# First down operands in the up weights' tiles, token sums ahead of a norm, and rows scaled on VectorE in an fp32 encoder block

## The chip, the cores and the metric

The kernel runs on one core of a Trainium2 chip. TensorE (PE in the profile) multiplies, VectorE (DVE) and ScalarE (ACT) do the elementwise work, GpSimd (POOL) raises the sums of the norms to a power, and SyncE's queue (SP) issues nearly all transfers between HBM and the core's memory. The metric is the device time of one execution, in microseconds (us).

## The reference

One encoder block on 2048 tokens of 1024 numbers, with 16 meta tokens ahead of them, all in fp32 (depth 1):

```python
for i in range(DEPTH):
    hn = rms_norm(h, g_mix[i])
    proj = hn @ w_in[i]                       # q, k, v and u, 512 + 256 + 256 + 512 wide
    ...                                       # axial rope, attention, Fourier mixing
    mixed = concatenate([rms_norm(attn, g_attn_out[i]), rms_norm(four, g_fourier_out[i])])
    h = h + mixed @ w_out[i]
    m = rms_norm(h, g_mlp[i])
    h = h + square(relu(m @ w_up[i])) @ w_down[i]      # 1024 -> 4096 -> 1024
return rms_norm(h, g_final)[:, N_META:]
```

## The kernel before

Every fp32 product is made of three matmuls on two halves of each operand: `split` writes hi, a cast on ACT (L64), and lo, the rest, a subtraction on DVE (L65); `mm3` then issues hi by hi (L74), one cross product (L75) and the other (L76). An operand of 128x1024 numbers is one cast and one subtraction.

The tokens stand in four blocks of 512. First come the projections, the Fourier part and attention; the MLP of blocks 0 and 1 is interleaved with attention (`head`, `up`, `down`), its weights coming through `wtile`: a ring of raw tiles (wr), and rings of four hi (wh) and four lo (wl) tiles. Blocks 2 and 3 are done last and together, each of the two products of the MLP as a Strassen scheme of seven forms, whose order is `ORDER = "1265734"`:

- `flip` scales the rows of blocks 2 and 3 by their norm (L1128), transposes them on PE (L1132) and evicts them (L1133) into b11, b21, b12, b22. Form operands bf1 to bf7 are splits of these four and of sums of them; bf3 to bf7 lie in a pool `sl` that takes the place of the pools `mp` and `wp`, and so over the rows of block 1.
- `final(1)` norms block 1 (DVE, L1036, with rs from POOL) and stores it to out.
- the up stage: 8 groups g of 512 columns of w_up, in each 7 forms of 24 matmuls (ux, uy in PSUM); the weights of a form come from `up_weights` (raw tiles R0 and R1, sums us1 and us2, halves wuh and wul, all in pool `sp`). Copies p1, p5, p6 (ACT, L1219) and sums c, s make the squared activations, which SP stores to s_d in HBM.
- the down stage: 4 groups of 7 forms of 48 matmuls (dx, dy). `down_operands` loads s_d (raw a) and w_down (raw d11, d21, d12, d22) and splits them into rings of five (ah, al, bh, bl). Sums d11 and t2 come between. DVE adds each finished product to hs (L1356), the rows of blocks 2 and 3. At the end each row is normed with g_final (gf) and stored.

A scheduler orders each engine's instructions; each engine then runs in its order, and SP's queue issues in its own, waiting with each DMA for the one eight before it. A tile that takes the place of another waits for that one's last readers, its store included.

Of the kernel before, what the change touches and what calls it, by code (L numbers as in the profile page):

```python
# [129 lines left out]
def encoder_block(ctx: ExitStack, tc: tile.TileContext, x, meta, w_in, w_f,  # L130
# [893 lines left out]
    def final(b):  # L1024
        b0, n = BLOCKS[b]
        hs = H.pop(b)
        gfin = load_gfin(b)
        for t in range(2 * n):
            ss = MT[b, "f"][t]
            sm = mp.tile([P, 1], F32, name=f"fsm_{b}_{t}", tag="hsm", bufs=2)  # L1030
            nc.vector.tensor_tensor(sm, ss[:, 0:1], ss[:, 1:2], op=ALU.add)
            rs = rstd_of(mp, sm, 1, D, "m2" if b == 2 else "m")
            r0 = (2 * b0 + t) * P
            for i in range(2):
                v = hs[t][:, i * 512:(i + 1) * 512]
# [131 lines left out]
    bt = {n: sl.tile([P, 2, 4, 512], R32, name="bf" + n, tag="bf" + n) for n in ORDER[2:]}  # L1167
    two = (slice(0, 2), slice(2, 4))
# [313 lines left out]
```

## Time and profile before

| | |
|---|---|
| median of 3 runs | 2391.14 us (2390.89 to 2393.72) |
| profiled execution, its own time | 2395.55 us |
| its span | 2393.8 us |
| PE busy | 2324.0 us (97%) |
| DVE busy | 1748.4 us (73%) |
| ACT busy | 1302.5 us (54%) |
| POOL busy | 161.4 us (7%) |

The span runs from the first to the last instruction that the profiler saw. Matmuls are pipelined, so a row of 0.39 us starts 0.23 us after the one ahead of it. A wait in brackets is idle time of that engine just ahead of the row, with what ended it. PEclk is the share of the full TensorE clock that was granted.

### The profile page before, as it was taken

How to read it: one execution, taken by the hardware profiler on the slowest of the kernel's cores; microseconds unless marked ns; L12 is line 12 of the kernel's file. 1: busy time of each engine (PE TensorE's matmuls, PEld its weight loads, DVE VectorE, ACT ScalarE, POOL GpSimd, SP SyncE). 2: the span in 40 equal slices, each digit the busy share in tenths (PEclk: the TensorE clock that was granted, in tenths of full speed). 3: DMA queues.
4: the chain of work that ended last, by engine and by line, in shares of the span. 5: the costliest groups of instructions: out<-in, count | busy, mean ns of one | idle time of the engine just before them, and what ended most of it. 6: DMA issues, size and time to landing. Idle time of an engine off the chain costs nothing.

```text
span 2393.8 us, 33707 instructions
## 1 busy us (share of the span) xinstructions
PE 2324.0 (97%) x12326; PEld 1977.8 (83%) x12326; DVE 1748.4 (73%) x2953; ACT 1302.5 (54%) x2529; POOL 161.4 (7%) x207
## 2 busy tenths in 40 slices
PE   8999989999999999999999999999979999799998
PEld 7889889788788888888888888888868888688886
DVE  5434678998687877787887887877484656487786
ACT  6434345654666656566765665665755555433343
POOL 2212120101100000000000000000000000000000
PEclk9999999999999999999999999999989999899999
DMA  6333152434334222234242334223334445755431
GB/s 210 108 98 114 45 169 56 153 115 150 128 88 117 74 77 70 76 102 118 70 150 80 133 106 126 67 71 114 138 110 163 150 145 178 266 185 169 139 123 71
DMA packets 169446, 288.64 MB, mean 121 GB/s; under 512 B 14160, under 2 KB 63024, under 8 KB 169280
## 3 DMA queue, kind: packets, MB, share of 16 engines
q1 hardware_dynamic: 149472, 256.34, 32.6%
q0 software_dynamic: 19808, 30.15, 4.8%
q8 instruction: 97, 1.59, 0.3%
q14 instruction: 69, 0.57, 0.1%
HBM read 216.93 MB, written 69.50 MB: 120 GB/s over the span
## 4 chain that ended last, share of the span: by engine, by line
PE 76%; DVE 4%; ACT 3%; DMA 2%; issue 1%; POOL 1%; SPq 0%; POOLq 0%; DVEq 0%; ACTq 0%
PE pup L74 5%; PE pup L75 5%; PE pup L76 5%; PE pdn L74 5%; PE pdn L75 5%; PE pdn L76 4%; PE s L74 2%; PE s L76 2%; PE s L75 2%; PE ux L74 2%; PE ux L76 2%; PE ux L75 2%; PE dx L74 2%; PE dx L75 2%; PE dx L76 2%; PE o L757 2%
## 5 line engine op out<-in xcount | busy, mean ns | idle before, releaser
L74 PE MATMUL pdn<-wh_dn,ah 128*128 128x512 f32 x512 | 202.6, 397 | 0.0
L74 PE MATMUL pup<-mT,wh_up 128*128 128x512 f32 x512 | 202.0, 396 | 0.7 <-ACT mT L67 0.7
L75 PE MATMUL pdn<-wl_dn,ah 128*128 128x512 f32 x512 | 202.0, 394 | 0.0
L76 PE MATMUL pup<-mT,wl_up 128*128 128x512 f32 x512 | 201.7, 396 | 0.0
L75 PE MATMUL pup<-mT,wh_up 128*128 128x512 f32 x512 | 201.7, 394 | 0.0
L76 PE MATMUL pdn<-wh_dn,al 128*128 128x512 f32 x512 | 199.5, 392 | 0.0
L696 ACT COPY S<-s 128x512 f32<-128x512 f32 (+1 forms) x288 | 159.8, 559 | 62.7 <-PE s L76 42.4
L736 DVE TENSOR_TENSOR S<-S,mb 128x512 f32<-128x512 f32 (+1 forms) x288 | 185.9, 654 | 4.4 <-ACT mb L725 4.3
L741 ACT ACTIVATE S<-S 128x512 f32<-128x512 f32 (+1 forms) x264 | 156.0, 603 | 59.3 <-DVE S L736 58.1
L64 ACT CAST wh_up<-wr_up 128x512 fp32r<-128x512 f32 x128 | 79.4, 620 | 160.5 <-PE pdn L76 71.6
L74 PE MATMUL s<-q,kt 128*128 128x256 f32 (+1 forms) x544 | 159.2, 293 | 1.4 <-ACT S L696 1.4
L703 DVE TENSOR_TENSOR M<-M,S 128x512 f32<-128x512 f32 (+1 forms) x224 | 145.4, 649 | 14.4 <-ACT S L696 12.9
L76 PE MATMUL s<-q,kt 128*128 128x256 f32 (+1 forms) x544 | 154.9, 285 | 0.0
L75 PE MATMUL s<-q,kt 128*128 128x256 f32 (+1 forms) x544 | 154.4, 284 | 0.0
L65 DVE TENSOR_TENSOR wl_up<-wr_up,wh_up 128x512 fp32r<-128x512 f32 x128 | 87.6, 688 | 87.0 <-ACT wh_up L64 86.9
L64 ACT CAST ah<-a 128x1024 fp32r<-128x1024 f32 x56 | 58.7, 1051 | 162.1 <-issue 58.8
L65 DVE TENSOR_TENSOR wl_dn<-wr_dn,wh_dn 128x512 fp32r<-128x512 f32 x128 | 88.0, 688 | 71.6 <-ACT wh_dn L64 70.6
L64 ACT CAST wh_dn<-wr_dn 128x512 fp32r<-128x512 f32 x128 | 79.3, 619 | 105.2 <-PE pdn L76 55.9
L763 DVE TENSOR_TENSOR acc<-acc,S 128x512 f32<-128x512 f32 x168 | 115.2, 686 | 1.7 <-ACT S L741 1.7
L65 DVE TENSOR_TENSOR pl<-S,ph 128x512 fp32r<-128x512 f32 x168 | 114.6, 686 | 2.0 <-ACT ph L64 1.4
L74 PE MATMUL dx<-bh,ah 128*128 128x512 f32 x256 | 100.7, 394 | 14.3 <-ACT bh L64 14.3
L74 PE MATMUL o<-ph,vt 128*128 128x256 f32 x384 | 111.5, 290 | 2.1 <-ACT ph L64 2.0
(310 smaller groups left out, 6818.7 us busy)
## 6 DMA issues: line engine op xcount, KB each, us to landing
wr_up<-in_w_up_dram SPq DMA_DIRECT2D x128, 256.0 KB, 2.8
wr_dn<-in_w_down_dram SPq DMA_DIRECT2D x128, 256.0 KB, 2.7
a<-s_d SPq DMA_DIRECT2D x56, 512.0 KB, 3.8
R<-in_w_up_dram SPq DMA_DIRECT2D x16, 1024.0 KB, 5.5
s_d<-s SPq DMA_DIRECT2D x64, 256.0 KB, 2.0
d<-in_w_down_dram SPq DMA_DIRECT2D x32, 512.0 KB, 4.8
s_d<-c SPq DMA_DIRECT2D x48, 256.0 KB, 2.0
h<-h_d SPq DMA_DIRECT2D x20, 512.0 KB, 6.0
```

The costliest lines, as they stand in the source:

```text
L64: nc.scalar.copy(hi, src)
L65: nc.vector.tensor_tensor(lo, src, f32v(hi), op=ALU.subtract)
L74: nc.tensor.matmul(out, a[0], b[0], start=first, stop=False, skip_group_check=chain)
L75: nc.tensor.matmul(out, a[0], b[1], start=False, stop=False, skip_group_check=chain)
L76: nc.tensor.matmul(out, a[1], b[0], start=False, stop=last, skip_group_check=chain)
L696: nc.scalar.copy(S[:rows, :n], ps[:rows, :n])
L703: nc.vector.tensor_tensor(M[:rows, :n], M[:rows, :n], S[:rows], op=ALU.max)
L736: nc.vector.tensor_tensor(S, S, bc(s["mb"][:rows], [rows, n, 256]), op=ALU.subtract)
L741: nc.scalar.activation(p, S, AF.Exp, scale=ISQ)
L757: nc.tensor.matmul(s["O"], vt[t // 4][:, t % 4], p[:, e], start=t == 0, stop=False)
L763: nc.vector.tensor_tensor(acc, acc, p, op=ALU.add)
```

## The change

Three things are done. First, the operands of form 1 of the first down group are made while the last up group (g = 7) runs: the raw a1 and d11 are loaded into R0 and R1, which no further up weights need, and split into the tiles of wuh, wul, us1 and us2. Half of the rows hs is loaded during that group, too, and the gf loads stand behind the first operands' loads. The ring bh, bl of the down operands lies in a new pool `dr` over `sp`, allocated after form 1's products. Second, at the start of the up stage the sums of the token operands come ahead of `final(1)`, into an extra tile (b32 in the listings); g_final is loaded earlier, the first half of block 1's rows is multiplied by it ahead of the norm on DVE (L1163 after the change), and by rs on ACT (L1038), the second half as before on DVE (L1040). The forms are then split in the order 6, 5, 7, 3, 4. One more up form is made ahead (4 for 3). Third, `flip` scales its rows on DVE instead of ACT, and the raw weight ring has three tiles for four.

```diff
@@ in wtile (and in out_f alike)
-        raw = wp.tile([P, 512], F32, name="wr_" + name, tag="wr", bufs=4)
+        raw = wp.tile([P, 512], F32, name="wr_" + name, tag="wr", bufs=3)
@@ in final, now final(b, early=None)
-        gfin = load_gfin(b)
+        gfin = early or load_gfin(b)
...
-                nc.vector.scalar_tensor_tensor(v, v, rs, gfin[i], op0=ALU.mult, op1=ALU.mult)
+                if early and i == 0:
+                    nc.scalar.activation(v, v, AF.Copy, scale=rs)
+                else:
+                    nc.vector.scalar_tensor_tensor(v, v, rs, gfin[i], op0=ALU.mult, op1=ALU.mult)
@@ before and in flip
-    ready = [next(UW) for _ in range(3)]
+    ready = [next(UW) for _ in range(4)]
...
-            nc.scalar.activation(hs[t], hs[t], AF.Copy, scale=ms[t])
+            nc.vector.tensor_scalar(hs[t], hs[t], ms[t], None, op0=ALU.mult)
@@ the token operands
     mix2(down(1, 7, (0,)), flip(2, h2, (b11, b21)))
+    gfin = load_gfin(1)
+    for t in range(4):
+        nc.vector.tensor_tensor(H[1][t][:, :512], H[1][t][:, :512], gfin[0], op=ALU.mult)
...
-    b12, b22 = (rb.tile([P, 4, 512], F32, name=f"b{i}2", tag=f"b{i}2") for i in (1, 2))
+    b12, b22, b22t = (rb.tile([P, 4, 512], F32, name=f"b{i}2", tag=f"b{i}2") for i in (1, 2, 3))
     mix2(down(1, 7, (1,)), flip(3, H.pop(3), (b12, b22)))
     b_form("1", ...)
     b_form("2", ...)
-    final(1)
+    minus(b11, b12, b11)      # dst = a - b, in two halves
+    minus(b22t, b22, b11)
+    final(1, gfin)
     mp.release()
     wp.release()
...
-    for c in two:
-        nc.vector.tensor_tensor(b11[:, c], b12[:, c], b11[:, c], op=ALU.subtract)
-    b_form("3", bt["3"], b22)
-    for c in two:
-        nc.vector.tensor_tensor(b12[:, c], b22[:, c], b12[:, c], op=ALU.subtract)
-        nc.vector.tensor_tensor(b22[:, c], b22[:, c], b11[:, c], op=ALU.subtract)
-    b_form("6", bt["6"], b22)
-    b_form("5", bt["5"], b11)
-    b_form("7", bt["7"], b12)
-    for c in two:
-        nc.vector.tensor_tensor(b21[:, c], b21[:, c], b22[:, c], op=ALU.subtract)
-    b_form("4", bt["4"], b21)
+    b_form("6", bt["6"], b22t)
+    b_form("5", bt["5"], b11)
+    minus(b12, b22, b12)
+    b_form("7", bt["7"], b12)
+    b_form("3", bt["3"], b22)
+    minus(b21, b21, b22t)
     rb.release()
+    sl4 = Lines(tc.alloc_tile_pool(name="sl4", bufs=1, reuse_waits="tile"), small)
+    b_form("4", sl4.tile([P, 2, 4, 512], R32, name="bf4", tag="bf4"), b21)
@@ new, ahead of the up loop
+    def first_down():
+        a = sp.tile([P, 4, 512], F32, name="a1_0", tag="R0")
+        nc.sync.dma_start(a, s_d[0][:, 0])
+        w = sp.tile([P, 4, 512], F32, name="d11_0", tag="R1")
+        for h in range(2):
+            nc.sync.dma_start(w[:, 2 * h:2 * h + 2], w_down[...])
+        yield
+        for h in range(2):
+            for x, r in (("a", a), ("b", w)):
+                tags = ("us1", "us2") if h and x == "b" else ("wuh", "wul")
+                hi, lo = (sp.tile([P, 2, 512], R32, ...) for e, t in zip("hl", tags))
+                split(hi, lo, r[:, 2 * h:2 * h + 2])
+                FIRST.append((hi, lo))
+                yield
+        yield w
@@ in the up loop, after a form's matmuls are issued
+            elif g == 7:
+                next(first, None)
+                if name == "7":
+                    load_h(0)
@@ in down_operands (RING["b"] is a pool dr, made over sp after form 1 of group 0)
-            stationary("1")
-            load(1, 1)
+            if g:
+                stationary("1")
+                load(1, 1)
+            else:
+                raw[1, 1] = [w11[:, 0:2], w11[:, 2:4]]
             stationary("2")
...
-            yield form("1", raw[1, 1])
+            if g == 0:
+                t1 = [dn.tile([P, 2, 512], F32, name=f"d11_0_{h}", tag="d11", bufs=2) for h in range(2)]
+                sub(t1, raw[1, 2], raw[1, 1])
+            yield form("1", raw[1, 1]) if g else FIRST
             yield form("2", raw[2, 1])
@@ ahead of and in the down loop
-    for t in range(8):
-        nc.sync.dma_start(hs[t], h_d[8 + t])
+    DO = down_operands()
+    ready = [next(DO)]
+    load_h(1)
     gfin = ...
-    DO = down_operands()
-    ready = [next(DO) for _ in range(2)]
...
+                if "b" not in RING:
+                    sp.release()
+                    RING["b"] = dr = Lines(tc.alloc_tile_pool(name="dr", ...), small)
+                    ready.append(next(DO))
```

DVE at the end of the up stage and the start of the down stage, before (dx_0_0 is the first product of form 1 of group 0; al1, bl1 are the lo halves of form 1, al2, bl2 of form 2):

```order
L1225 TENSOR_TENSOR s4_7_1_21008<-c21_7_1_21004,s2_7_1_20965 128x512
L65 TENSOR_TENSOR al1_0_0_21060<-a1_0_0_21031,ah1_0_0_21059 128x1024
L65 TENSOR_TENSOR al1_0_1_21068<-a1_0_1_21033,ah1_0_1_21067 128x1024
L65 TENSOR_TENSOR bl1_0_0_21064<-d11_0_0_21035,bh1_0_0_21063 128x1024
L65 TENSOR_TENSOR bl1_0_1_21072<-d11_0_1_21037,bh1_0_1_21071 128x1024
L65 TENSOR_TENSOR al2_0_0_21076<-a2_0_0_21039,ah2_0_0_21075 128x1024
L65 TENSOR_TENSOR al2_0_1_21084<-a2_0_1_21041,ah2_0_1_21083 128x1024
L1356 TENSOR_TENSOR hs0_21017<-hs0_21017,dx_0_0_21099 128x512
L65 TENSOR_TENSOR bl2_0_0_21080<-d21_0_0_21043,bh2_0_0_21079 128x1024
L1356 TENSOR_TENSOR hs0_21017<-hs0_21017,dx_0_1_21112 128x512
```

And after the change:

```order
L1268 TENSOR_TENSOR s4_7_1_21038<-c21_7_1_21034,s2_7_1_20991 128x512
L1407 TENSOR_TENSOR hs0_20930<-hs0_20930,dx_0_0_21092 128x512
L1407 TENSOR_TENSOR hs0_20930<-hs0_20930,dx_0_1_21105 128x512
L1407 TENSOR_TENSOR hs0_20930<-hs0_20930,dx_0_2_21118 128x512
L65 TENSOR_TENSOR al2_0_0_21149<-a2_0_0_21051,ah2_0_0_21148 128x1024
L1407 TENSOR_TENSOR hs0_20930<-hs0_20930,dx_0_3_21131 128x512
L65 TENSOR_TENSOR al2_0_1_21157<-a2_0_1_21053,ah2_0_1_21156 128x1024
L1327 TENSOR_TENSOR d11_0_0_21071<-d12_0_0_21059,d11_0_20895 128x1024
L1327 TENSOR_TENSOR d11_0_1_21072<-d12_0_1_21061,d11_0_20895 128x1024
L1327 TENSOR_TENSOR t2_0_0_21164<-d22_0_0_21063,d11_0_0_21071 128x1024
L65 TENSOR_TENSOR bl2_0_0_21153<-d21_0_0_21055,bh2_0_0_21152 128x1024
L65 TENSOR_TENSOR bl2_0_1_21161<-d21_0_1_21057,bh2_0_1_21160 128x1024
```

The four lo halves of form 1 stood behind the last up sum (s4); now the last of them, al1_0_1, stands five rows above it, behind the addition c12_7_1 and ahead of three sums s, and the other three stand further up. The lo half bl2_0_0 now stands behind the sums d11 and t2, which came behind both bl2 before.

ACT at the start of the up stage, before (wuh are hi halves of up weights, bf of token operands, p1 the copies of form 1's products):

```order
L64 CAST wuh7_0_18820<-R0_0_18342 128x1024
L64 CAST wuh3_0_18859<-us2_0_18355 128x1024
L64 CAST bf3_18724<-b22_18521 128x1024 x2
L64 CAST bf5_18722<-b11_18370 128x1024 x2
L64 CAST bf7_18723<-b12_18520 128x1024
L64 CAST bf6_18721<-b22_18521 128x1024 x2
L64 CAST bf7_18723<-b12_18520 128x1024
L64 CAST wuh4_0_18893<-R1_0_18344 128x1024
L64 CAST bf4_18725<-b21_18371 128x1024 x2
L1219 COPY p1_0_0_18789<-ux_0_0_18759 128x512
```

And after the change:

```order
L64 CAST wuh7_0_18798<-R0_0_18342 128x1024
L1038 ACTIVATE h_1_0_10470<-h_1_0_10470,rs_m_18693 128x512
L1038 ACTIVATE h_1_1_10472<-h_1_1_10472,rs_m_18703 128x512
L1038 ACTIVATE h_1_2_10474<-h_1_2_10474,rs_m_18713 128x512
L1038 ACTIVATE h_1_3_10476<-h_1_3_10476,rs_m_18723 128x512
L64 CAST wuh3_0_18833<-us2_0_18355 128x1024
L64 CAST bf6_18734<-b32_18534 128x1024 x2
L64 CAST bf5_18735<-b11_18374 128x1024 x2
L64 CAST bf7_18736<-b12_18532 128x1024 x2
L64 CAST bf3_18737<-b22_18533 128x1024 x2
L64 CAST bf4_18762<-b21_18375 128x1024 x2
L64 CAST wuh4_0_18871<-R1_0_18344 128x1024
```

The forms 6, 7, 3 and 4 are all cast ahead of wuh4 and of the copies p1, form 4 no longer between wuh4 and p1, and four scales of block 1 (L1038) stand ahead of wuh3.

DVE in the same place, before (ms feeds the power on POOL whose result is rs; wul are lo halves of up weights):

```order
L1173 TENSOR_TENSOR b12_18520<-b22_18521,b12_18520 128x1024
L1036 SCALAR_TENSOR_TENSOR h_1_2_10474<-h_1_2_10474,rs_m_18700,gfin_1_0_18672 128x512
L1036 SCALAR_TENSOR_TENSOR h_1_2_10474<-h_1_2_10474,rs_m_18700,gfin_1_1_18673 128x512
L1036 SCALAR_TENSOR_TENSOR h_1_3_10476<-h_1_3_10476,rs_m_18710,gfin_1_0_18672 128x512
L1036 SCALAR_TENSOR_TENSOR h_1_3_10476<-h_1_3_10476,rs_m_18710,gfin_1_1_18673 128x512
L65 TENSOR_TENSOR wul7_0_18821<-R0_0_18342,wuh7_0_18820 128x1024
L65 TENSOR_TENSOR wul3_0_18860<-us2_0_18355,wuh3_0_18859 128x1024
L65 TENSOR_TENSOR bf3_18724<-b22_18521,bf3_18724 128x1024 x2
L1174 TENSOR_TENSOR b22_18521<-b22_18521,b11_18370 128x1024 x2
L65 TENSOR_TENSOR bf5_18722<-b11_18370,bf5_18722 128x1024
```

And after the change:

```order
L184 TENSOR_SCALAR ms_m_18711<-fsm_1_2_18709 128x1
L184 TENSOR_SCALAR ms_m_18721<-fsm_1_3_18719 128x1
L1174 TENSOR_TENSOR b21_18375<-b21_18375,b32_18534 128x1024
L1040 SCALAR_TENSOR_TENSOR h_1_2_10474<-h_1_2_10474,rs_m_18713,gfin_1_1_18521 128x512
L1040 SCALAR_TENSOR_TENSOR h_1_3_10476<-h_1_3_10476,rs_m_18723,gfin_1_1_18521 128x512
L65 TENSOR_TENSOR wul7_0_18799<-R0_0_18342,wuh7_0_18798 128x1024
L65 TENSOR_TENSOR wul3_0_18834<-us2_0_18355,wuh3_0_18833 128x1024
L65 TENSOR_TENSOR bf6_18734<-b32_18534,bf6_18734 128x1024 x2
L65 TENSOR_TENSOR bf5_18735<-b11_18374,bf5_18735 128x1024 x2
L65 TENSOR_TENSOR bf7_18736<-b12_18532,bf7_18736 128x1024 x2
```

Between the last rows of block 1 and the lo half of bf5 stood two halves of weights, two of bf3 and the two sums on L1174; now stand there the weights and the two of bf6. The last sums ahead of the norm of rows 2 and 3 are those of b21, which stood further down before.

## Rows read from the trace of the kernel before

**Rows 1.** The waits of PE, longest first, over the whole span.
```profile
PE dx L74 <- ACT bh L64: 14.3, 1, 14.3
...
PE pmt L1132 <- ACT h L1128: 0.4, 1, 0.4
```

**Rows 2.** Busy time by stretch: us, busy us of each engine, clock, DMA share, GB/s.
```profile
700.00:1180.00 480.00, 479.96 (x2632) 408.98 (x2632) 378.24 (x673) 290.17 (x560) 23.08 (x32) 1.00 0.31 91
1769.00:1780.00 11.00, 10.15 (x38) 8.21 (x39) 7.46 (x8) 6.79 (x12) 0.00 (x0) 0.84 0.43 144
2074.00:2081.00 7.00, 6.59 (x15) 4.74 (x16) 5.21 (x6) 5.39 (x6) 0.00 (x0) 0.51 1.04 387
2081.00:2371.00 290.00, 290.00 (x1281) 240.13 (x1280) 227.86 (x252) 108.87 (x125) 1.10 (x2) 1.00 0.44 144
```

**Rows 3.** Timeline of PE at the start of the down stage: start, length, instruction, wait.
```profile
2059.69 0.39 PE L76 MATMUL ux<-bf,wul 128*128 128x512 f32 x1
2074.37 1.22 PE L74 MATMUL dx<-bh,ah 128*128 128x512 f32 x2 [14.29 <-ACT bh L64]
...
2088.59 0.39 PE L74 MATMUL dy<-bh,ah 128*128 128x512 f32 x1
```

**Rows 4.** Timeline of ACT there.
```profile
2070.53 1.05 ACT L64 CAST ah<-a 128x1024 fp32r<-128x1024 f32 x1 [9.15 <-DMA a<-s_d]
...
2080.11 1.05 ACT L64 CAST bh<-d 128x1024 fp32r<-128x1024 f32 x1 [0.36 <-DMA d<-in_w_down_dram]
```

**Rows 5.** Timeline of PE at the start of the up stage.
```profile
1755.34 1.22 PE L74 MATMUL uy<-bf,wuh 128*128 128x512 f32 x2 [6.59 <-ACT bf L64]
1759.38 0.80 PE L75 MATMUL uy<-bf,wuh 128*128 128x512 f32 x1 [2.82 <-DVE bf L65]
...
1766.17 0.39 PE L76 MATMUL uy<-bf,wul 128*128 128x512 f32 x1
1769.85 0.50 PE L74 MATMUL ux<-bf,wuh 128*128 128x512 f32 x1 [3.28 <-ACT p L1219]
```

**Rows 6.** Timeline of ACT there.
```profile
1754.24 5.98 ACT L64 CAST bf<-b 128x1024 fp32r<-128x1024 f32 x6 [2.74 <-DMA out_dram<-h]
1766.37 1.04 ACT L64 CAST wuh<-R 128x1024 fp32r<-128x1024 f32 x1 [6.16 <-PE uy L75]
...
1769.22 1.06 ACT L1219 COPY p<-ux 128x512 f32<-128x512 f32 x2
```

**Rows 7.** Timeline of DVE as the up stage ends.
```profile
2058.00 0.69 DVE L1236 TENSOR_TENSOR s<-c,c 128x512 f32<-128x512 f32 x1 [1.36 <-ACT c L1190]
```

**Rows 8.** Timeline of SP's queue at the start of the down stage.
```profile
2062.67 1.70 SPq L1314 DMA_DIRECT2D gf<-in_g_final_dram  x2
```

**Rows 9.** The page's DMA issues, whole span: KB each, median us to landing.
```profile
wr_up<-in_w_up_dram SPq DMA_DIRECT2D x128, 256.0 KB, 2.8
...
a<-s_d SPq DMA_DIRECT2D x56, 512.0 KB, 3.8
```

**Rows 10.** Timeline of DVE at the start of the up stage.
```profile
1730.68 0.69 DVE L65 TENSOR_TENSOR wl_dn<-wr_dn,wh_dn 128x512 fp32r<-128x512 f32 x1 [10.03 <-ACT wh_dn L64]
...
1735.06 2.62 DVE L1013 TENSOR_TENSOR h<-h,pdn 128x512 f32<-128x512 f32 x4
...
1741.14 0.21 DVE L184 TENSOR_SCALAR ms_m<-fsm 128x1 f32<-128x1 f32 x2
...
1742.92 2.74 DVE L1036 SCALAR_TENSOR_TENSOR h<-h,rs_m,gfin 128x512 f32<-128x512 f32 x4 [0.44 <-POOL rs_m L186]
...
1748.63 2.74 DVE L1036 SCALAR_TENSOR_TENSOR h<-h,rs_m,gfin 128x512 f32<-128x512 f32 x4 [0.44 <-POOL rs_m L186]
...
1758.10 6.90 DVE L65 TENSOR_TENSOR bf<-b,bf 128x1024 fp32r<-128x1024 f32 x6
```

**Rows 11.** DMA issues while block one is stored.
```profile
out_dram<-h SPq DMA_DIRECT2D x8, 256.0 KB, 2.1
```

**Rows 12.** ACT groups by line: the scale in flip; busy us, mean ns.
```profile
L1128 ACT ACTIVATE h<-h,rs_m 128x1024 f32<-128x1024 f32 x8 | 9.0, 1143 | 1.0 <-DMA h_d<-h 1.0
```

More of the change, by code (lines that the diff above doesn't have):

```diff
@@ L825, in out_f @@
             for h in range(2):
-                raw = wp.tile([P, 512], F32, name=f"wfr{k}_{h}", tag="wr", bufs=4)
+                raw = wp.tile([P, 512], F32, name=f"wfr{k}_{h}", tag="wr", bufs=3)
                 nc.sync.dma_start(raw, w_out[512 + k * P:512 + (k + 1) * P, h * 512:(h + 1) * 512])
@@ L1022, in load_gfin, with final @@
         return gfin
-    def final(b):
+    def final(b, early=None):
         b0, n = BLOCKS[b]
         hs = H.pop(b)
-        gfin = load_gfin(b)
+        gfin = early or load_gfin(b)
         for t in range(2 * n):
@@ L1162, in encoder_block, with minus @@
     b_form("2", ey.tile([P, 2, 4, 512], R32, name="bf2", tag="e1"), b21)
-    final(1)
+    two = (slice(0, 2), slice(2, 4))
+    def minus(dst, a, b):
+        for c in two:
+            nc.vector.tensor_tensor(dst[:, c], a[:, c], b[:, c], op=ALU.subtract)
+    minus(b11, b12, b11)
+    minus(b22t, b22, b11)
+    final(1, gfin)
     mp.release()
@@ L1166, in encoder_block @@
     sl = Lines(tc.alloc_tile_pool(name="sl", bufs=1, reuse_waits="tile"), small)
[L1167 to L1180 removed]
+    bt = {n: sl.tile([P, 2, 4, 512], R32, name="bf" + n, tag="bf" + n) for n in "6573"}
+    b_form("6", bt["6"], b22t)
+    b_form("5", bt["5"], b11)
+    minus(b12, b22, b12)
+    b_form("7", bt["7"], b12)
+    b_form("3", bt["3"], b22)
+    minus(b21, b21, b22t)
     rb.release()
+    sl4 = Lines(tc.alloc_tile_pool(name="sl4", bufs=1, reuse_waits="tile"), small)
+    b_form("4", sl4.tile([P, 2, 4, 512], R32, name="bf4", tag="bf4"), b21)
     ra.release()
@@ L1190, in relu2, with load_h @@
         nc.scalar.square(dst, dst)
+    FIRST = []
+    hs = []
+    def load_h(i):
+        HS = ey.tile([P, 4, D], F32, name=f"hs{i}", tag=f"e{i}")
+        for t in range(4):
+            nc.sync.dma_start(HS[:, t], h_d[8 + 4 * i + t])
+            hs.append(HS[:, t])
+    def first_down():
[3 more added lines that the diff above has]
+        for h in range(2):
+            nc.sync.dma_start(w[:, 2 * h:2 * h + 2], w_down[h * 512:h * 512 + 256, :512].rearrange("(p r) d -> r p d", r=P))
+        yield
+        for h in range(2):
+            for x, r in (("a", a), ("b", w)):
+                tags = ("us1", "us2") if h and x == "b" else ("wuh", "wul")
+                hi, lo = (sp.tile([P, 2, 512], R32, name=f"{x}{e}1_0_{h}", tag=t, bufs=4 if t in ("wuh", "wul") else 1)
+                          for e, t in zip("hl", tags))
+                split(hi, lo, r[:, 2 * h:2 * h + 2])
+                FIRST.append((hi, lo))
+                yield
+        yield w
+    first = first_down()
     for g in range(8):
@@ L1242, in encoder_block @@
                         keep("7", p, s3)
+    *_, w11 = first
     pc.release()
-    sp.release()
+    sl4.release()
     sl.release()
     dn = Lines(tc.alloc_tile_pool(name="dn", bufs=1, reuse_waits="tile"), small)
+    RING = {"a": dn}
     def down_operands():
@@ L1272, in form @@
                     for x, r in (("a", S[name][h]), ("b", src[h])):
-                        hi, lo = (dn.tile([P, 2, 512], R32, name=f"{x}{e}{name}_{g}_{h}", tag=x + e, bufs=5)
+                        hi, lo = (RING[x].tile([P, 2, 512], R32, name=f"{x}{e}{name}_{g}_{h}", tag=x + e, bufs=5)
                                   for e in "hl")
@@ L1360, in encoder_block @@
                     products(t)
+                if "b" not in RING:
+                    sp.release()
+                    RING["b"] = dr = Lines(tc.alloc_tile_pool(name="dr", bufs=1, side="right", reuse_waits="tile"), small)
+                    ready.append(next(DO))
                 w = next(DO, None)
@@ L1379, in encoder_block @@
     dn.release()
+    dr.release()
     yp.release()
```

8 lines of the change are left out of this document (4 added, 4 removed).

## The prediction

> **What bounds the kernel now.** The page comes first: PE is busy 97% of a span of 2393.8 us, so only PE's idle time and half-clock stretches can be won. The waits of PE [rows 1] then put most of it at one place, 14.3 us ahead of the down stage's first matmul, and almost none (0.4) at the transposes of `flip`. The busy time by stretch [rows 2] shows what needs no further look: PE has 479.96 of 480 us in the MLP stretch from 700 on and all of 2081 to 2371, where 1281 matmuls take 290.00 us, 0.2264 each. It also prices the clock: after a wait PE runs at a granted clock of 0.51 of 2.4 GHz, that is at its 1.2 GHz level, for some us. From 2074 to 2081, behind the 14.29 us wait, 15 matmuls took 6.59 us where full clock gives 3.4, a loss of 3.2; from 1769 to 1780, behind 3.28 us, 38 took 10.15 for 8.6, a loss of 1.5.
>
> The timelines name the causes. At the down stage PE ends the up stage at 2059.9 (2059.69 and a pace) and starts again at 2074.37 [rows 3]; ACT waits from the last up work to 2070.53 for the load of a1, then casts eight operands as they land, the first at 2070.53 and the eighth at 2080.11, one per 1.37 us [rows 4]. At the up stage PE waits 6.59 us for the hi half of bf5, 2.82 for its lo half, and 3.28 for the copy p1 [rows 5]. ACT could not cast bf5 before 1754.24, because block 1's rows, which lie under it, were being stored; p1 stood behind wuh4 and bf4 [rows 6].
>
> **The down stage.** Form 1's operands are now made ahead. In the listing of DVE the last of them, al1_0_1, stands ahead of a sum s that waited 1.36 us for ACT at 2058.00 [rows 7]; at 1.14 us it fits there and is ready at 2057.9, 2 us before PE is. The three others and four casts, some 8 us on two engines, spread over seven forms of 5.4 us; DVE is busy 73% of the span, so I cost them at nothing. If al1_0_1 slips behind the last up sums, form 1 starts some 3 us late. PE goes on without a wait and at full clock: 48 matmuls at 0.2264, 10.9 us, end at 2070.8.
>
> Form 2 is late next. Its loads take the place of gf in SP's queue, at 2062.67 [rows 8]; with the median of 3.8 us to landing [rows 9] and 1.37 from one to the next the seventh, d22_0, is there at 2074.7. With the delay of before (issue at 2064.4, behind gf, cast at 2070.53: 6.1 us) it is 2077.0. But DVE holds it longer. In the listing bl2_0_0 stands behind the addition of dx_0_3, al2_0_1, two halves of d11 and t2_0_0. The last product of form 1 is out at 2071.1, the addition (0.69) ends at 2071.8, and five instructions at 1.14 (a row of six took 6.90 [rows 10]) end at 2077.5. PE has issued three L74 by 2071.5, so it waits 6.0 us and then runs at the lower clock: 45 matmuls are 10.2 us, plus a loss between 1.5 and 3.2, for which I take 2 since 6 us lies nearer to 3.28 than to 14.29. Form 2 ends at 2089.7. Before it started at 2088.59 [rows 3] and ended at 2099.5. Gain 9.8 us. With the late landing t2_0_0 starts at 2077.0 instead of 2075.2, which takes 1.8 off. Forms 6 and 5 have their lo halves 3 to 6 us after form 2's, ahead of 2089.7. The rows hs are loaded during the last up group as before.
>
> **The up stage.** DVE's chain [rows 10], step by step: one more sum of 1.14 ahead of L1013, which ended at 1737.7, so 1738.8; bf2 lo, b11 and two of b32 (4.6), 1743.4; fsm 0.2, b12, ms 0.2, b12, 1746.1. From ms to the norm's first product it took 1741.14 to 1742.92, 1.8 us, so rs is there at 1746.6, and two L1040 (0.69 each) end at 1747.9. Then fsm, b21, ms, b21 end at 1750.6, rs of rows 2 and 3 comes at 1751.1, the last L1040 ends at 1752.5. Before it was 1748.63 plus 2.74, 1751.4: the last store leaves 1.1 us later, although two instructions per row became one. The stores land 2.1 us after issue [rows 11], so the hi half of bf5 starts at 1755.4 instead of 1754.24, and the first wait of PE grows by 1.1. The lo half goes the other way: behind 1752.5 stand wul7, wul3 and two of bf6, no longer two of bf3 and two sums besides, so it ends at 1758.2 and not 1759.3. The pair of waits shrinks by 1.1, and so form 5 ends 1.1 earlier. Form 6 waits for p1: ACT has cast bf5, bf7, bf3 and bf4 (8 at 1.0 from 1755.4) by 1763.4, ahead of wuh4, which waits for form 5 until 1765.3; p1 starts at 1766.2 and PE at 1766.9 instead of 1769.85. Gain 3.0 us, the clock left alone. It is 1.0 if bf5 comes a further 2 us later, and 4.5 if the shorter last wait (1.5 us) costs no clock.
>
> **What I cost at nothing.** The scale in `flip` is 1.143 us on ACT, eight times [rows 12]; the trace has no such instruction on DVE at this size. The nearest rows are one scaling of 512 elements by two operands at 0.69 and two-tensor instructions of 1024 at 1.22; I take 1.22. DVE stood idle 10.03 us up to 1730.68 [rows 10], which holds the eight scales and the four new products with g_final (2.7) but for about 2 us, and those can end as late as PE's transposes allow. So 0, between a loss of 2 and the gain of the 0.4 in rows 1. The Trainium skill, VectorE: DVE Perf Modes, section on the perf-mode tier table, says that a scale of one fp32 tensor runs twice as fast as a sum of two. No run here shows it yet; by that rule the eight take some 5 us (an estimate), the 0.4 goes, and the sum is 13.2 instead of 12.8.
>
> The ring of three raw tiles: a load lands in 2.8 us [rows 9], and a weight tile serves 12 matmuls, 2.72 us; three tiles ahead are 8.2 us, so the load stays hidden. The load of the last down tile of block 1 now stands behind both g_final loads on SP; PE needs it some 10 us later. Cost 0, up to 3 where block starts crowd the queue.
>
> **Sum.** 9.8 + 3.0 = 12.8. The profiled execution took 2395.55 us, 4.4 above the median of the runs shown, 2391.14. So 2382.8 under the profiler, 2378.3 as a median; I say 2378. Bounds: the down stage 7 to 11, the up stage 1 to 4.5, the rest -3 to 0.4: 5 to 16.
>
> **The rivals.**
> - The whole down wait goes: DVE or the loads run ahead of my chain, and form 2 follows form 1 at full clock. Then 14.3 plus 3.2 are won, with 3 at the up stage 20.5: 2371. For it: the loads alone would allow form 2's first lo half by about 2074. Against it: the order of DVE, in which bl2_0_0 can't pass d11 and t2.
> - The early operands are of less use than that: al1_0_1 behind the last up sums (3 us and a clock loss of 1.5), loads at the old delay (1.8), the up stage at its lower end (2 less). The gain falls to 4.5: 2386.6. For it speaks that every one of these has a row with the bad value; against it that each alone leaves 8.
> - Slower: the weight ring. If a tile were loaded only when the one ahead is done, each of 288 tiles would cost 2.80 instead of 2.72 us, 23 us; less 12.8 this is 2401. It decides if the raw tile is released more than 5.4 us after its load landed (8.2 less 2.8). For it: SP's queue is in order and shared, so one late release holds all behind it. Against it: PE has no idle time between 700 and 1180 [rows 2], and the cast, which frees the raw tile with the subtraction, runs as soon as a hi tile is free.
>
> **How the numbers follow.** Forecast 0.62 (2375 to 2382), full gain 0.10, small gain 0.21, slower 0.07. The range of 2372 to 2387 leaves out the ring and the tails on both sides. A difference below 0.2%, 4.8 us, counts as none, so faster ends at 2386.4; of the small-gain case 0.08 lies below it and 0.13 in the band. Faster 0.80, same 0.13, slower 0.07.
>
> **What would show it.** In the changed kernel PE passes from the up to the down stage without a wait; a wait of about 6 us for bl on DVE stands three matmuls into form 2. At the up stage the waits of uy are about 7.7 and 0.6, that of ux 1.5. The MLP stretch has no new wait of PE for casts. I am wrong if form 2 starts without a wait, if form 1 waits, or if waits for wh or wl appear before 1700.

## The result, and the profile after

| | before | after |
|---|---|---|
| median | 2391.01 us (2390.08 to 2393.72, 4 runs) | 2376.49 us (2374.75 to 2380.12, 4 runs) |
| ratio | | 0.9939, 95% interval 0.9922 to 0.9957 |
| profiled execution, its own time | 2395.55 us | 2375.63 us |
| its span | 2393.8 us | 2373.8 us |
| PE busy | 97% | 98% |

The median fell by 14.5 us; 2378 (2372 to 2387) was forecast. The waits of PE after the change, over the whole span, longest first (engine, matmul, what it waited for: total us, times, longest):

```profile
...
PE uy L74 <- ACT bf L64: 8.2, 1, 8.2
PE dy L75 <- DVE bl L65: 5.7, 1, 5.7
...
PE dy L74 <- ACT bh L64: 1.5, 1, 1.5
PE ux L74 <- ACT p L1262: 1.4, 1, 1.4
```

The 14.3 us of dx [rows 1] are gone; in their place stand two waits of dy, of 1.5 and 5.7, one form later. At the start of the up stage there were three waits of 6.59, 2.82 and 3.28 [rows 5], and there are two. PE's timeline shows the down stage's start; it answers to [rows 3]:

```profile
2047.31 0.39 PE L76 MATMUL ux<-bf,wul 128*128 128x512 f32 x1
2047.53 0.39 PE L74 MATMUL dx<-bh,ah 128*128 128x512 f32 x1
...
2060.12 0.98 PE L74 MATMUL dy<-bh,ah 128*128 128x512 f32 x3 [1.54 <-ACT bh L64]
...
2066.82 0.80 PE L75 MATMUL dy<-bl,ah 128*128 128x512 f32 x1 [5.73 <-DVE bl L65]
2067.42 0.63 PE L76 MATMUL dy<-bh,al 128*128 128x512 f32 x1
```

Form 1 follows the last up matmul at the usual pace of 0.22 us. Form 2 then waits, first for a cast, after three L74 for its lo half, and goes on at half clock: the next row has 0.63 us where full clock has 0.39, and the granted clock was 0.50 from 2066.80 to 2070.00. The same stretch on SP, ACT and DVE (SP answers to [rows 8], ACT to [rows 4]):

```profile
2050.38 1.71 SPq L1312 DMA_DIRECT2D a<-s_d  x2
2052.15 4.15 SPq L1305 DMA_DIRECT2D d<-in_w_down_dram  x6
```

```profile
2056.31 1.05 ACT L64 CAST ah<-a 128x1024 fp32r<-128x1024 f32 x1 [7.32 <-DMA a<-s_d]
...
2059.02 1.04 ACT L64 CAST bh<-d 128x1024 fp32r<-128x1024 f32 x1 [0.34 <-DMA d<-in_w_down_dram]
```

```profile
2044.31 1.22 DVE L65 TENSOR_TENSOR al<-a,ah 128x1024 fp32r<-128x1024 f32 x1
...
2061.65 2.57 DVE L1327 TENSOR_TENSOR d<-d,d 128x1024 f32<-128x1024 f32 x2 [1.22 <-DMA d<-in_w_down_dram]
2064.41 1.22 DVE L1327 TENSOR_TENSOR t<-d,d 128x1024 f32<-128x1024 f32 x1 [0.18 <-DMA d<-in_w_down_dram]
2065.55 2.35 DVE L65 TENSOR_TENSOR bl<-d,bh 128x1024 fp32r<-128x1024 f32 x2
```

The last lo half of form 1 runs at 2044.31, ahead of the last sums, 3.2 us before PE starts on dx. The first load of form 2 is issued at 2050.38 and cast at 2056.31, 5.9 us later. On DVE bl2 stands behind d11 and t2, which wait 1.22 and 0.18 us for loads.

The start of the up stage, PE and then ACT; they answer to [rows 5] and [rows 6]:

```profile
1749.45 1.22 PE L74 MATMUL uy<-bf,wuh 128*128 128x512 f32 x2 [8.15 <-ACT bf L64]
...
1759.08 0.50 PE L74 MATMUL ux<-bf,wuh 128*128 128x512 f32 x1 [1.39 <-ACT p L1262]
```

```profile
1748.36 7.74 ACT L64 CAST bf<-b 128x1024 fp32r<-128x1024 f32 x8 [1.49 <-DMA out_dram<-h]
1757.50 1.04 ACT L64 CAST wuh<-R 128x1024 fp32r<-128x1024 f32 x1 [1.41 <-PE uy L75]
1758.45 1.07 ACT L1262 COPY p<-ux 128x512 f32<-128x512 f32 x2
```

The casts of bf5 still begin when block 1's store has landed, but p1 now has only wuh4 ahead of it, and the second wait (2.82 for the lo half) is gone. Busy time by stretch (us, then busy us and instructions of PE, PEld, DVE, ACT, POOL, then granted clock, DMA share, GB/s), one at the up and one at the down stage:

```profile
1759.00:1770.00 11.00, 10.92 (x48) 9.06 (x49) 6.34 (x7) 5.91 (x11) 0.00 (x0) 1.00 0.43 144
2067.00:2074.00 7.00, 7.00 (x21) 5.56 (x22) 7.00 (x7) 4.92 (x5) 0.00 (x0) 0.66 1.05 407
```

Behind the 1.39 us wait the clock stays at 1.00 (48 matmuls in 10.92 us), where behind 3.28 it had been 0.84 [rows 2]. Behind the 5.73 us wait it is 0.66.

### Where the 14.5 us came from

Each row below is one profiled execution. The columns are distances on PE's timeline, in us: from the first attention product (pa) to the first score (s), whose code is the same in all; from the first matmul of the Fourier output to the first of the attention output; from the last attention product to the first up product (the scale is in it); from the first to the last ux; from the last ux to the last dx.

| kernel | pa to s | Fourier output | to first ux | up stage | down stage |
|---|---|---|---|---|---|
| before | 25.82 | 181.26 | 80.72 | 322.11 | 322.44 |
| after | 22.39 | 177.78 | 79.87 | 317.15 | 314.83 |
| e_down | 22.89 | 179.76 | 80.74 | 322.65 | 315.41 |
| e_up | 23.40 | 178.05 | 80.24 | 317.96 | 320.87 |
| e_ring_scale | 23.02 | 178.95 | 80.15 | 323.71 | 321.03 |
| e_ring | 23.56 | 179.01 | 80.50 | 321.65 | 322.07 |
| e_scaleact | 21.99 | 178.14 | 81.07 | 318.76 | 314.35 |
| x_pool | 24.15 | 178.31 | 80.03 | 317.93 | 317.83 |
| x_order | 25.13 | 178.37 | 79.82 | 316.99 | 308.59 |

The two profiled executions of before and after differ by 19.9 us, 5.4 more than the medians. Of that 3.4 lies in the first column, where no code differs and the other twelve kernels have 22.0 to 25.1: chance. The rest of the table is the change: down stage 7.6, up stage 5.0, Fourier output 3.5 by this pair of single executions.

### The profile page after: what moved, and what is told of

The parts are those of the page before. It is cut to its first block, busy times and chain, and to the rows that moved or that the text cites. A ratio compares the mean times of both kernels' runs of the same rounds, so it can differ in the third digit from the quotient of the medians.

```text
span 2373.8 us, 33706 instructions
## 1 busy us (share of the span) xinstructions
PE 2319.4 (98%) x12326; PEld 1976.1 (83%) x12326; DVE 1750.6 (74%) x2961; ACT 1295.2 (55%) x2525; POOL 160.4 (7%) x207
## 4 chain that ended last, share of the span: by engine, by line
PE 78%; DVE 3%; ACT 2%; DMA 2%; issue 1%; POOL 1%; SPq 0%; POOLq 0%; DVEq 0%; ACTq 0%
PE pdn L74 5%; PE pdn L75 5%; PE pdn L76 5%; PE pup L74 5%; PE pup L75 5%; PE pup L76 5%; PE s L74 3%; PE s L76 3%; PE s L75 3%; PE ux L74 2%; PE ux L76 2%; PE ux L75 2%; PE o L757 2%; PE dx L76 2%; PE dx L75 2%; PE dx L74 2%
## 5 line engine op out<-in xcount | busy, mean ns | idle before, releaser
L74 PE MATMUL pdn<-wh_dn,ah 128*128 128x512 f32 x512 | 202.9, 397 | 0.0
L74 PE MATMUL pup<-mT,wh_up 128*128 128x512 f32 x512 | 201.6, 396 | 0.6 <-ACT mT L67 0.6
L74 PE MATMUL s<-q,kt 128*128 128x256 f32 (+1 forms) x544 | 159.2, 293 | 0.4 <-ACT S L696 0.4
L74 PE MATMUL o<-ph,vt 128*128 128x256 f32 x384 | 111.5, 290 | 2.1 <-ACT ph L64 2.0
L76 PEld LDWEIGHTS pdn<-wh_dn,al 128*128 128x128 f32 x512 | 96.1, 188 | 19.5
```

What stands on the lines that cost most here:

```text
L74: nc.tensor.matmul(out, a[0], b[0], start=first, stop=False, skip_group_check=chain)
L76: nc.tensor.matmul(out, a[1], b[0], start=False, stop=last, skip_group_check=chain)
```

## The experiments

### One part at a time

**e_down** is before with the down part alone, **e_up** is after without it:

```diff
@@ e_down, against before (and the hunks of first_down, load_h, RING and dr as in the change)
+            elif g == 7:
+                next(first, None)
@@ e_up, against after: the same taken out again
-            yield form("1", raw[1, 1]) if g else FIRST
+            yield form("1", raw[1, 1])
```

> The kernel before with the down-stage part alone (form 1's first down operands made during the last up group; ring of four, scale on ScalarE and norm order as before). Theory: the whole wait ahead of the down stage goes and returns in part inside form 2, so the gain is that of the changed kernel's trace at this place, 7.6 us: about 2383, with PE waiting some 1.5 us for bh and 5.5 to 6 us for bl in form 2. Rival: part of the saving at this place depends on the up part (operands ready in time only because the up stage runs differently); then form 1 waits and the gain is under 5, above 2386.

> The changed kernel without the down-stage part (ring of three, scale on VectorE, sums ahead of the norm and split g_final stay). Theory: it gains what the two traces differ by from the start of the up stage's form 1 to the end of the up stage, 5.0 us, and up to 1 from the flip: 2385 to 2386, with the 14 us wait at the down stage unchanged. Rival: the up part's gain is taken back at the down stage, since the last stores and loads set its start, not PE: then within 1.5 us of 2391.

e_down: 2384.76 us, ratio to before 0.9967 (0.9956 to 0.9978). e_up: 2382.37, 0.9962 (0.995 to 0.9975). The waits of PE in e_down, then in e_up:

```profile
...
PE uy L74 <- ACT bf L64: 6.6, 1, 6.6
PE dy L75 <- DVE bl L65: 5.8, 1, 5.8
...
PE ux L74 <- ACT p L1252: 3.3, 1, 3.3
...
PE uy L75 <- DVE bf L65: 2.8, 1, 2.8
```

```profile
PE dx L74 <- ACT bh L64: 13.9, 1, 13.9
...
PE uy L74 <- ACT bf L64: 8.4, 1, 8.4
...
PE ux L74 <- ACT p L1229: 1.4, 1, 1.4
```

Each part removes its own waits and leaves the other's. e_down came out as expected. e_up was faster than expected by some 3 us, and its table row says where: 4 us at the up stage, and 3 at the Fourier output, which only the ring of three touches.

### The ring and the scale

**e_ring_scale** is before with the third part alone; **e_ring** has the ring without the scale; **e_scaleact** is after with the scale back on ACT.

```diff
@@ e_ring_scale; e_ring has the first two lines (in wtile and out_f) only
-        raw = wp.tile([P, 512], F32, name="wr_" + name, tag="wr", bufs=4)
+        raw = wp.tile([P, 512], F32, name="wr_" + name, tag="wr", bufs=3)
...
-            nc.scalar.activation(hs[t], hs[t], AF.Copy, scale=ms[t])
+            nc.vector.tensor_scalar(hs[t], hs[t], ms[t], None, op0=ALU.mult)
@@ e_scaleact, against after: the second pair in reverse
```

> The kernel before with the raw weight ring of three and the scale of flip on VectorE, nothing else. The profiled executions differ by some 7 us ahead of the up stage. Theory: that is chance of two executions, these two edits move the median by less than 1.5 us either way: 2389.5 to 2392.5. Rival: the ring and the order that the scheduler makes with it are worth 2 to 4 us around the Fourier output and the first block's weights: 2387 to 2389.

> The changed kernel with the scale of flip back on ScalarE. Theory: the scale is off the critical path on either engine and costs at most the 0.4 us wait of PE seen before and some tenths in the flip: 2376 to 2378. Rival: VectorE's extra 5 to 10 us in that stretch delay the chain of sums ahead of the norm, so that ScalarE would be better by 1 to 2 us: 2374 to 2375.5.

> The kernel before with the raw weight ring of three tiles for four and nothing else (the scale of flip stays on ScalarE). Ring and scale together made the median 3.9 us shorter. Theory from the stretches of seven profiled executions: the ring with its other order of loads is worth 2 to 2.5 us at the Fourier output (the time from the first matmul of pof to the first of poa was 181.3 and 179.8 us with four tiles, 177.8 to 178.9 with three), the scale 0.7 us: 2389 to 2390 here. Rival: all of it is the scale on VectorE: 2391 to 2392 here.

e_ring_scale: 2387.99 us, 0.9984 (0.9975 to 0.9993), the time of its rival. e_ring: 2389.43, 0.9986 (0.9978 to 0.9995), as its theory had it. e_scaleact: 2378.37, 0.9945 (0.9931 to 0.9958), which can't be told from after. So the ring of three, which I had at nothing or a loss, gains 1 to 5 us; the Fourier output takes 181.26 and 179.76 us with four tiles (before, e_down) and 177.8 to 179.0 in the eleven kernels with three. The scale is worth 0.65 us by the column to the first ux: a mean of 80.77 over five kernels with it on ACT, 80.12 over nine with it on DVE. The two groups just overlap (80.50 and 80.60), and timing alone doesn't show it. Nor does the next stage always keep it: e_ring and e_ring_scale differ in the scale alone, and their up stages take 321.65 and 323.71 us. The scale's line on DVE, after (min/median/max ns of one, first and last start):

```profile
L1132 DVE TENSOR_SCALAR h<-h,rs_m x8: 748/753/754, 1705.7 to 1714.8; 128x1024 f32<-128x1024 f32 x8
```

0.753 us, not the 1.22 that I took. The Trainium skill, VectorE: DVE Perf Modes, section on the perf-mode tier table, by which one fp32 tensor scaled runs twice as fast as two summed, agrees in kind; the row has 0.62 of the time, not half.

Why three tiles are better than four was asked once more. With three, SP issues the loads of the first two x tiles (xo) together, ahead of most weight tiles of the Fourier output; with four the second stands behind four more of them. With three (after) SP's timeline has both in one row, at 421.84; before has

```profile
424.49 0.33 SPq L833 DMA_DIRECT2D xo<-in_x_dram  x1
431.20 3.77 SPq L827 DMA_DIRECT2D wfr<-in_w_out_dram  x4
435.03 0.42 SPq L833 DMA_DIRECT2D xo<-in_x_dram  x1
```

**e_xo** is before, ring of four, with these two loads moved ahead:

```diff
+        xts = {}
+        def load_x(t):
+            xts[t] = op_.tile([P, D], F32, name=f"xo_{t}", tag="xo", bufs=2)
+            nc.sync.dma_start(xts[t], x[t * P:(t + 1) * P, :])
+        load_x(0)
+        load_x(1)
...
-            xt = op_.tile([P, D], F32, name=f"xo_{t}", tag="xo", bufs=2)
-            nc.sync.dma_start(xt, x[t * P:(t + 1) * P, :])
+            if t > 1:
+                load_x(t)
+            xt = xts[t]
```

> The kernel before, with its ring of four for the weights of the Fourier output left alone, but with the loads of the first two x tiles of that output issued on SP ahead of those weights' loads. Theory that the gain of the ring of three comes from the x loads standing earlier in SP's queue: the stretch from the first matmul of the Fourier output to the first of its attention output falls from 181.3 us to 178 to 179, and the median to 2389 to 2390. Rival, that the order of these loads is not what the ring of three changed for the better: the stretch stays at 180 to 181, the median at 2391 to 2392.

2391.45 us, 0.9997 (0.9988 to 1.0006): the rival's time, but the theory's stretch, 178.05 us. The edit did more than it should. SP's timeline around it:

```profile
421.68 0.80 SPq L828 DMA_DIRECT2D xo<-in_x_dram  x2
422.54 12.22 SPq L835 DMA_DIRECT2D wfr<-in_w_out_dram  x8
```

The x loads wait for their place until 421.68, and now all eight weight tiles wait behind them; in before the first went out at 376.40 and three more from 401.15 on. The Fourier output starts later by what it is shorter: from the first score to its first matmul it takes 96.0 us, 92.5 in before, and the two stretches together take 274.1 and 273.8. The order of loads is not all that three tiles change, either: before and the eleven kernels with three have the same 958 matmuls in this stretch, but those with three have them in another order on PE (e_xo has 954). Whether the order of loads or that of the engines makes the ring's gain is not settled.

### What holds the rest of the up stage

**x_up** is after with the places of bf3 and bf5 exchanged, so that bf5 no longer lies over the last rows stored; with bf5 split ahead of bf6; and with bf4 cast on DVE, so that ACT is free for p1:

```diff
-    bt = {n: sl.tile([P, 2, 4, 512], R32, name="bf" + n, tag="bf" + n) for n in "6573"}
+    bt = {n: sl.tile([P, 2, 4, 512], R32, name="bf" + n, tag="bf" + n) for n in "6375"}
...
-    b_form("4", sl4.tile([P, 2, 4, 512], R32, name="bf4", tag="bf4"), b21)
...
+    for c in two:
+        nc.vector.tensor_copy(b4[:, 0:4][:, c], b21[:, c])
+        nc.vector.tensor_tensor(b4[:, 4:8][:, c], b21[:, c], b4[:, 0:4][:, c], op=ALU.subtract)
```

> The changed kernel with bf5 in the place of the pool that no stored row of block one lies under (its place and that of bf3 exchanged), split ahead of bf6, and bf4's hi half cast on VectorE so that it does not stand ahead of p1. Theory: the first wait of the up stage (8.15 us for bf5's hi half) is the way of block one's rows through the norm and the stores; without it ScalarE casts bf5 behind wuh3, 3.4 us earlier, VectorE's lo half comes 3.1 us earlier, and PE's two waits shrink by about 3: 3 us under the changed kernel's time. Rival: VectorE's chain of sums and norm products is what counts, the stores only end with it; then bf5's lo half moves by a few tenths and the gain is under 1 us.

2376.80 us, 0.9939 (0.9926 to 0.9951), as after. PE, DVE and ACT there:

```profile
1749.37 1.22 PE L74 MATMUL uy<-bf,wuh 128*128 128x512 f32 x2 [4.63 <-ACT bf L64]
...
1767.45 0.50 PE L74 MATMUL ux<-bf,wuh 128*128 128x512 f32 x1 [2.09 <-ACT p L1266]
```

```profile
1760.26 1.29 DVE L1194 CAST bf<-b 128x1024 fp32r<-128x1024 f32 x2
1761.46 2.35 DVE L1195 TENSOR_TENSOR bf<-b,bf 128x1024 fp32r<-128x1024 f32 x2
1763.73 1.28 DVE L1277 TENSOR_TENSOR c<-uy,p 128x512 f32<-128x512 f32 x2
```

```profile
1764.45 0.63 ACT L1203 ACTIVATE c<-c 128x512 f32<-128x512 f32 x1 [4.39 <-DVE c L1277]
...
1766.83 0.57 ACT L1266 COPY p<-ux 128x512 f32<-128x512 f32 x1
```

The wait for bf5 falls from 8.2 to 4.6 us, and comes back later: the casts of bf4 on DVE hold the sums c, ACT's relus wait 4.39 us for these, and the copy p behind them comes 2.09 us late; 28 matmuls then take 7.95 us for the 6.3 of full clock. The work that was taken from ACT sits on the path by way of DVE.

### What holds form 2

By the theory it is the order on DVE: d11, t2 and their loads ahead of bl2. Two ways to take them away. **x_pool** gives group 0's sums to GpSimd:

```diff
-                sub(t1, raw[1, 2], raw[1, 1])
+                for h in range(2):
+                    nc.gpsimd.tensor_tensor(t1[h], raw[1, 2][h], raw[1, 1][h], op=ALU.subtract)
@@ and t2 and t3 of g == 0 alike
```

> The changed kernel with the sums d11, t2 and t3 of the first down group on GpSimd instead of VectorE, so that bl2 does not stand behind them. Theory: form 2's 5.7 us wait is VectorE's order; bl2_0_0 then follows al2_0_1, PE waits some 1.5 us for bh and 0.5 to 1 us more, and the gain is 5 us plus up to 2 of half clock, if GpSimd ends t2 within 12 us: 5 to 7 us under the changed kernel's time. Rival: the loads set the pace; then the wait moves to form 6, which waits for t2 or a6, and less than 2 us are won.

2379.56 us, 0.9946 (0.9934 to 0.9959): no gain. PE, GpSimd and DVE (on GpSimd L1351 makes t2 and L1357 t3):

```profile
2062.95 0.73 PE L74 MATMUL dy<-bh,ah 128*128 128x512 f32 x2 [1.55 <-ACT bh L64]
2064.45 0.50 PE L75 MATMUL dy<-bl,ah 128*128 128x512 f32 x1 [0.77 <-DVE bl L65]
...
2080.21 0.50 PE L74 MATMUL dx<-bh,ah 128*128 128x512 f32 x1 [3.40 <-ACT ah L64]
...
2082.71 0.79 PE L76 MATMUL dx<-bh,al 128*128 128x512 f32 x1 [1.77 <-DVE al L65]
```

```profile
2070.08 2.38 POOL L1351 TENSOR_TENSOR t<-d,d 128x1024 f32<-128x1024 f32 x1
2072.43 2.40 POOL L1357 TENSOR_TENSOR d<-d,d 128x1024 f32<-128x1024 f32 x1
2074.79 3.34 POOL L1351 TENSOR_TENSOR t<-d,d 128x1024 f32<-128x1024 f32 x1
```

```profile
2073.58 2.32 DVE L65 TENSOR_TENSOR bl<-t,bh 128x1024 fp32r<-128x1024 f32 x1 [8.05 <-ACT bh L64]
2079.24 2.28 DVE L65 TENSOR_TENSOR bl<-t,bh 128x1024 fp32r<-128x1024 f32 x1 [3.34 <-ACT bh L64]
```

Form 2's long wait is gone (0.77 for 5.73), so the cause is right. But a sum takes 2.4 us on GpSimd, and the t2 that form 6 needs comes later than DVE made it: the wait has moved one form on. The four waits are 7.5 us together, 7.3 in after, and the clock falls twice (0.74 from 2064.45 to 2071.00, 0.57 from 2082.00 to 2090.00); the down stage takes 317.8 us, 3.0 more than in after. The second half of t2 stands on GpSimd behind a half of t3, which form 7 needs later, so this run does not tell the price of the slower engine from that of this order. **x_both**, x_up and x_pool together, was to show whether the two add up.

> Both of the above in one kernel. Theory: the gains add, 8 to 10 us under the changed kernel's time, 2367 to 2369. Rival: one or both fall to under 2 us, 2372 to 2376.

2377.92 us, 0.9943 (0.993 to 0.9955); form 6 waits 5.06 and 1.28 us. They don't. **a_again**, after unchanged, ran beside these three:

> The changed kernel itself on this chip, for comparison with the others: 2374.5 to 2378.5, and its profiled execution the same waits as the first one's.

2376.74 us, 0.9932 (0.9918 to 0.9946).

**x_order** leaves every sum on DVE and changes their order: form 2's operands are split ahead of d11 and t2, those from the weights into R0 and into the fourth pair of wuh and wul tiles, which the ring dr need not yet cover (the tile pad keeps it off R0 and R1).

```diff
...
+                R0 = sp.tile([P, 2, 2, 512], R32, name="b2_0", tag="R0")
+                got2 = [part("a", 0, S["2"][0], dn, ("ah", "al"), 5)]
+                split(R0[:, 0], R0[:, 1], raw[2, 1][0])
+                got2.append((R0[:, 0], R0[:, 1]))
+                got2.append(part("a", 1, S["2"][1], dn, ("ah", "al"), 5))
+                got2.append(part("b", 1, raw[2, 1][1], sp, ("wuh", "wul"), 4))
                 t1 = [dn.tile([P, 2, 512], F32, name=f"d11_0_{h}", tag="d11", bufs=2) for h in range(2)]
...
-            yield form("2", raw[2, 1])
+            yield form("2", raw[2, 1]) if g else got2
...
+                    dr.tile([P, 2, 4, 512], F32, name="pad", tag="pad")
```

> The changed kernel with form 2's b operands of the first down group in the up weights' tiles too (R0 and the fourth tiles of wuh and wul) and so made ahead of the sums d11 and t2 on VectorE, where they stood behind them; the down ring lies over the tiles behind R0 and R1. No other instruction is added. Theory: form 2's wait for bl is VectorE's order alone, since with the sums on GpSimd it shrank from 5.7 to 0.8 us, and what undid that was GpSimd's 2.4 to 2.8 us for each sum, which form 6 waited for. With VectorE's order PE starts form 2's second kind of product at about 2061.5 instead of 2066.8, form 6 waits up to 1 us for bl6: 4 to 5 us under the changed kernel's time. Rival: the loads are the limit, and form 6 waits for a6 or t2 as long as form 2 did: within 1 us of the changed kernel.

2372.71 us (2369.05 to 2376.16), 0.9917 (0.9904 to 0.993), 4 us below after's rerun, a_again, but with intervals that overlap: the timings alone don't show the gain. By the stage table the down stage is 6.2 us shorter than in after. PE, DVE, and the stretch by busy time:

```profile
2061.58 1.20 PE L74 MATMUL dy<-b,ah 128*128 128x512 f32 x4 [1.53 <-ACT b L64]
2063.10 0.50 PE L75 MATMUL dy<-b,ah 128*128 128x512 f32 x1 [0.32 <-DVE b L65]
...
2075.45 0.50 PE L75 MATMUL dx<-bl,ah 128*128 128x512 f32 x1 [1.17 <-DVE bl L65]
```

```profile
2061.82 1.22 DVE L65 TENSOR_TENSOR b<-d,b 128x1024 fp32r<-128x1024 f32 x1
2062.96 1.22 DVE L65 TENSOR_TENSOR bl<-d,bh 128x1024 fp32r<-128x1024 f32 x1
2064.09 2.35 DVE L1327 TENSOR_TENSOR d<-d,d 128x1024 f32<-128x1024 f32 x2
```

```profile
2064.00:2073.00 9.00, 9.00 (x42) 7.42 (x41) 8.79 (x10) 4.36 (x5) 0.00 (x0) 1.00 1.01 394
```

With bl2 ahead of d11 the 5.73 us and the half clock behind them are gone: the wait is DVE's order. What is left is 1.53 us for a cast behind the loads and 0.32, and form 6 waits 1.17; the clock stays at 1.00 behind them. **x_order_up** adds the places and the order of bf from x_up, bf4 staying on ACT:

```diff
-    bt = {n: sl.tile([P, 2, 4, 512], R32, name="bf" + n, tag="bf" + n) for n in "6573"}
-    b_form("6", bt["6"], b22t)
+    bt = {n: sl.tile([P, 2, 4, 512], R32, name="bf" + n, tag="bf" + n) for n in "6375"}
     b_form("5", bt["5"], b11)
+    b_form("6", bt["6"], b22t)
```

> The same, and at the up stage bf5 in a place over no stored row and split ahead of bf6, with bf4 on ScalarE as in the changed kernel. In the listing bf4's casts stand between wuh4 and p1. Theory: form 5 comes 3 us earlier, p1 2 us later behind bf4, so form 6 starts 0.9 us earlier; VectorE's additions c11 start no later than before, so nothing is given back behind it: 0.5 to 1 us under the kernel without it. Rival: as with bf4 on VectorE, the copy p6 behind c11 takes all of it back: 0.

2370.82 us (2370.18 to 2373.48), 0.9911 (0.9898 to 0.9923): the lowest median, though not apart from x_order. bf5 is waited for 4.7 us and p1 3.3, behind bf4; the up stage takes 317.86 us, no less than in after. The medians of x_order and x_order_up lie below those of the two kernels compared here, clear of before, not of after.

## Why the prediction was right

The time came out 1.5 us below the forecast. The mechanisms were the ones named, but their sizes were off: the down stage's term was 2.2 us too large, the up stage's 2.0 too small, and the ring and the scale, put at nothing, gave some 2.6 by the table. That they cancel to within 2 us is luck.

- **What bounds it: right.** Both large parts gained where PE had waited, and the other stages moved by 0.9 us or less, but for the Fourier output and the first column of the table.
- **Form 1 without a wait: right,** in after and e_down. al1_0_1 stands where the listing had it, ahead of a sum that waits.
- **Form 2 waits for bl2 behind d11 and t2: right in cause, mis-sized.** Forecast were 6.0 us of wait and 2 of clock; 7.27 (1.54 and 5.73) and 3.0 were measured: form 1 ends at 2058.40 (48 matmuls of 0.2264 from 2047.53), form 6 starts at 2079.49, and of these 21.1 us full clock takes 10.9. What failed is the load: d11 waited 1.22 us for its one and t2 0.18, where my chain had no wait. I took the median of 3.8 us to landing [rows 9]; the first load behind the switch needed 5.9 to its cast. That is the 6.1 of the old place, which I had worked out and kept as a bound of 1.8 us. The term was 9.8 and measured 7.6 (7.0 in e_down), inside its bounds of 7 to 11. Both numbers were at hand; the one from the same place in the program was the better, the page's median being over 56 loads of the whole stage. And of the clock's price I took 2, near the lower end; the other end, 3.2, was the nearer.
- **The up stage: right in cause, too small.** uy was to wait 7.7 and 0.6, ux 1.5; they wait 8.15, 0 and 1.39. The waits fell by 3.15 (12.69 to 9.54), as forecast. The 1.5 us of clock behind the third wait also went; I had that as the upper bound of 4.5. The stretch is 5.0 us shorter, 0.5 above that bound.
- **The ring of three at 0, with a loss as its bound: wrong.** It gained 1 to 5 us by e_ring. The rival that lets it hold up the weights finds nothing for it in any run. Why it gains stays open: the order of SP's loads and that of the engines' work both changed with it.
- **The scale at 0: 0.65 us gained up to the first ux,** by the table, not by the timings, and not shown for the whole; the duration I took was too long by 0.47, and most of the eight ran ahead of the idle stretch [rows 10] into which I had put them.
- **Sum.** By the stages 7.6 + 5.0 + about 2 (the two profiles with four tiles against the eleven with three) + 0.65 is 15.3; the median gives 14.5, 12.8 was forecast. What the up stage gave beyond its term, and the terms left at nothing, paid what the down stage lacked.
- **The rivals.** The whole down wait didn't go, since form 2's order held; x_order shows that most of it goes when that order does: its down stage is 13.8 us shorter than before, of the 17.5 that this rival counted. The small gain fell out: of its three parts only the old load delay came.

## What to carry to other kernels

When a stall goes, the next instruction in the same queue sets the gain: read in the listing what the new first waiter stands behind, and price it with the delay of the same place in the program, not with a median over the whole span. A sum that only a later form needs should be issued behind the operands that the next form needs; here that did more than giving the sums to GpSimd (down stage 308.6 us against 317.8). A term costed at nothing deserves a bound on both sides: here the ring of three, bounded as a loss alone, paid 1 to 5 us.

## What the runs showed of the hardware

- While GpSimd runs a two-tensor instruction, one on DVE takes 2.28 to 2.32 us for its 1.22, and GpSimd's next takes 3.34 for 2.38 (rows of x_pool). The times fit turns: DVE's at 2073.58 ends at 2075.90, 1.07 behind the end of GpSimd's at 2074.83, and GpSimd's of 2074.79 is longer by the 1.0 from there. The Trainium skill, SBUF — State Buffer, section SBUF: two separate sides, says that the two share a port pair that one holds for a whole instruction; the rows agree.
- The clock's price is not told by one wait's length alone in these runs: behind 1.39 us (after), behind 1.53 and 0.32 and behind 1.17 (x_order) the granted clock stayed at 1.00. Behind 2.09 (x_up: 0.79 from 1767.40 to 1775.35) and behind 1.55 and 0.77 (x_pool: 0.74 from 2064.45 to 2071.00) it fell, at some 1.6 us each (28 matmuls in 7.95 us, 22 in 6.55); behind 1.54 and 5.73 (after) it cost 3.0.
